# Second up projection as seven quarter products, with weight sums made by adding transfers

## The chip, the cores and the metric

One Trainium2 chip; the program runs on one of its cores. The metric is the device time of one execution in microseconds (us), less is better. Three runs of the kernel before gave a median of 1473.71 us (1473.31 to 1474.12).

The engines of the core are named as the profile names them: PE (TensorE, matmuls; PEld is its weight loads), DVE (VectorE), ACT (ScalarE), POOL (GpSimd) and SP (SyncE, which only issues transfers here). Each executes its own list of instructions in order and waits on semaphores for the others.

## What is computed

Two layers over 512 latent tokens and 256 context tokens of width 1024. Layer 0 mixes by a short gated convolution and a wide (31 taps) convolution module, layer 1 by windowed attention; each is followed by a ConvFFN. The change is in the ConvFFN of layer 1, which has latent tokens only. Cut to that:

```python
D_MODEL, SEQ, D_FF = 1024, 512, 2816

def conv_ffn(h, w_up, conv, w_down):
    u = dwconv(h @ w_up, conv)              # h: 512 x 1024, w_up: 1024 x 5632, conv: 3 taps per channel
    a, g = jnp.split(u, 2, axis=-1)
    return (jax.nn.silu(g) * a) @ w_down    # w_down: 2816 x 1024

x = x + g2 * conv_ffn(modulate(rmsnorm(x, norm_ffn[l]), sh2, sc2), w_up[l], w_conv_ffn[l], w_down[l])
```

All inputs are float32. In layer 0 the part that will matter is the wide convolution of the mixer: `u = v_b * sigmoid(gate_b)`, `dwconv(u, conv_b) + bias`, then a layer norm.

## The kernel before

**Layout.** Activations lie transposed: channels on the 128 partitions, tokens along the free dimension. A width of 1024 is eight k tiles. For accuracy every operand of a large matmul is split into a high and a low part (`split`, lines 157 to 160: ACT casts to the reduced type, DVE subtracts), and each product is three matmuls: low x high, high x low, high x high (`mm3`, lines 174 to 179). In the profile these are L177, L178 and L179.

**Weights.** `weights` (lines 162 to 168) has SP load a 128 x 1024 tile into one of three `wraw` buffers and splits it into `whi` and `wlo`. Loads run ahead as far as the three buffers let them.

**Second FFN** (`ffn` with l = 1). The inner width of 2816 is 22 pairs; pair f has an `a` tile and a `g` tile of the up projection. An up tile is 8 k tiles x 3 = 24 matmuls with 512 columns into one PSUM slot. There are eight slots (`turn` hands them out in turn). The first three pairs are computed half by half, while the tokens' halves are still being normalised (`side_by_side`, L208, L209 and L212). For each tile `conv3` applies the three taps (ACT L368, then DVE L370 twice), ACT takes silu of `g` (L704), DVE multiplies (L705) and `pair` splits the product into `gh` and `gl`. The pairs fall into five groups (`GROUPS`); after the first pair of the next group, `down` computes all eight tiles of the down projection for the group before, and `gate_in` (L360) adds each into `x`. The last group goes through `project`, which ends in the final norm. At the start of each FFN, `mod_rows` computes the modulation rows on DVE (`junk`, L254), from rows that SP loads.

**Layer 0.** `start` loads x and the modulation weights (`wmod`, line 222) and computes `h`. `glu` (lines 558 to 584) makes for each of four channel tiles j the padded input `ub`: POOL clears its three margins (line 568), DVE writes the body (line 570), ACT starts the convolution with tap 0 (`cacc`, line 575, which reads the margins), and 30 further taps follow on DVE (line 578). When tiles 0 and 1 are done POOL adds them into `cs` (line 584). `conv_norm` multiplies `cs` by a matrix of ones on PE (line 622) for the mean. `inverse` (lines 286 to 302) computes a reciprocal root, in most places on POOL (`ry`, L296).

**Order.** The program is written in source order; a scheduler then sets the order of each engine's list from the dependencies and from its own estimate of durations, so an instruction can be moved far from its place in the source. POOL issues no transfers in this kernel.

## Time and profile before

| what | value |
|---|---|
| median of three runs | 1473.71 us |
| profiled execution, its own time | 1473.53 us |
| its span (first to last instruction) | 1471.8 us |
| PE, busy share of the span | 98% |
| DVE, ACT, POOL | 70%, 41%, 3% |
| layer 0 up to its FFN | about 0 to 312 us |
| first FFN | about 312 to 836 us |
| attention | about 836 to 1072 us |
| second FFN, with the end of the attention's output | about 1072 to 1472 us |

An instruction's row has its start and duration; matmuls are pipelined, so the interval from one start to the next tells what one costs, not the duration of 0.28 or 0.39 us. In brackets stands the idle time of that engine before the instruction and what ended it. DMA share is the mean busy share of the core's 16 DMA engines. PEclk is the granted clock of PE, 1.00 being 2.4 GHz.

### The profile page before, as it was taken

How to read it: one execution, taken by the hardware profiler on the slowest of the kernel's cores; microseconds unless marked ns; L12 is line 12 of the kernel's file. 1: busy time of each engine (PE TensorE's matmuls, PEld its weight loads, DVE VectorE, ACT ScalarE, POOL GpSimd, SP SyncE). 2: the span in 40 equal slices, each digit the busy share in tenths (PEclk: the TensorE clock that was granted, in tenths of full speed). 3: DMA queues.
4: the chain of work that ended last, by engine and by line, in shares of the span. 5: the costliest groups of instructions: out<-in, count | busy, mean ns of one | idle time of the engine just before them, and what ended most of it. 6: DMA issues, size and time to landing. Idle time of an engine off the chain costs nothing.

```text
span 1471.8 us, 21937 instructions
## 1 busy us (share of the span) xinstructions
PE 1435.4 (98%) x8786; PEld 1228.8 (83%) x8786; DVE 1024.4 (70%) x1635; ACT 596.9 (41%) x983; POOL 47.8 (3%) x186
## 2 busy tenths in 40 slices
PE   5999999999999999999999999999999999999997
PEld 3888888888888888888888878768799888888887
DVE  6699998689977756456434689786676865655456
ACT  5421224463223223133123475786764442424245
POOL 0000001110000000000000110010001000000000
PEclk9999999999999999999999999999999999999999
DMA  9325433134544532333211324011155333233222
GB/s 374 111 70 173 158 115 130 31 113 146 168 132 127 186 106 81 120 125 91 81 47 43 106 91 125 14 40 58 42 174 163 90 112 98 84 114 97 94 80 74
DMA packets 52709, 161.25 MB, mean 110 GB/s; under 512 B 6400, under 2 KB 6528, under 8 KB 52480
## 3 DMA queue, kind: packets, MB, share of 16 engines
q1 hardware_dynamic: 52608, 159.87, 33.4%
q8 instruction: 68, 1.11, 0.3%
q14 instruction: 33, 0.27, 0.1%
HBM read 155.13 MB, written 2.10 MB: 107 GB/s over the span
## 4 chain that ended last, share of the span: by engine, by line
PE 91%; DVE 4%; ACT 2%; issue 1%; DMA 1%; POOL 1%; DVEq 0%; SPq 0%; ACTq 0%; POOLq 0%
PE slot L177 21%; PE slot L178 21%; PE slot L179 21%; PE av L178 3%; PE av L177 3%; PE av L179 3%; PE av L929 2%; PE pt L919 2%; PE s L900 2%; PE pt L179 2%; PE pt L178 2%; PE pt L177 2%; PE slot L226 1%; PE slot L212 1%; PE slot L208 1%
## 5 line engine op out<-in xcount | busy, mean ns | idle before, releaser
L177 PE MATMUL slot<-h,wlo 128*128 128x512 f32 (+1 forms) x1192 | 410.5, 346 | 2.2 <-DVE ub L570 1.2
L178 PE MATMUL slot<-h,whi 128*128 128x512 f32 (+1 forms) x1192 | 410.8, 345 | 0.2 <-DVE h L350 0.2
L179 PE MATMUL slot<-h,whi 128*128 128x512 f32 (+1 forms) x1192 | 410.8, 345 | 0.0
L159 ACT CAST whi<-wraw 128x1024 fp32r<-128x1024 f32 (+2 forms) x215 | 192.2, 902 | 208.5 <-PE slot L179 109.3
L177 PEld LDWEIGHTS slot<-h,wlo 128*128 128x128 f32 x1192 | 223.5, 188 | 34.3 <-issue 2.0
L178 PEld LDWEIGHTS slot<-h,whi 128*128 128x128 f32 x1192 | 224.1, 188 | 29.0 <-DVE h L350 0.5
L179 PEld LDWEIGHTS slot<-h,whi 128*128 128x128 f32 x1192 | 224.1, 188 | 27.6
L160 DVE TENSOR_TENSOR wlo<-wraw,whi 128x1024 fp32r<-128x1024 f32 (+2 forms) x215 | 222.2, 1040 | 25.1 <-ACT whi L159 24.6
L370 DVE SCALAR_TENSOR_TENSOR cf<-slot,par,cf 128x775 f32<-128x775 f32 (+1 forms) x132 | 122.7, 932 | 136.5 <-ACT cf L368 136.0
L177 PE MATMUL slot<-gh,wlo 128*128 128x512 f32 (+1 forms) x459 | 156.7, 342 | 0.7 <-DVE x L360 0.4
L178 PE MATMUL slot<-gl,whi 128*128 128x512 f32 (+1 forms) x459 | 155.5, 339 | 0.0
L179 PE MATMUL slot<-gh,whi 128*128 128x512 f32 (+1 forms) x459 | 155.1, 339 | 0.0
L368 ACT ACTIVATE cf<-slot,par 128x776 f32<-128x776 f32 (+1 forms) x66 | 55.3, 837 | 243.1 <-PE slot L179 230.7
L360 DVE SCALAR_TENSOR_TENSOR x<-slot,mod,x 128x256 f32<-128x256 f32 (+1 forms) x139 | 81.8, 618 | 73.6 <-PE slot L179 73.4
L578 DVE SCALAR_TENSOR_TENSOR cacc<-ub,par,cacc 128x783 f32<-128x783 f32 x120 | 118.6, 1040 | 0.2
L254 DVE CUSTOM_DVE_ANT_0 junk<-wmod,cb 128x1024 bf16<-128x1024 f32 x80 | 97.7, 1221 | 10.2 <-DMA wmod<-in_wmt 6.6
L177 PEld LDWEIGHTS slot<-gh,wlo 128*128 128x128 f32 x459 | 86.1, 188 | 12.0 <-DVE wlo L160 0.7
L178 PEld LDWEIGHTS slot<-gl,whi 128*128 128x128 f32 x459 | 86.4, 188 | 10.3 <-DVE mod L235 0.2
L179 PEld LDWEIGHTS slot<-gh,whi 128*128 128x128 f32 x459 | 86.4, 188 | 10.1
L907 DVE CUSTOM_DVE_ANT_0 sm<-s,mask,nsink 128x640 f32<-128x640 f32 (+1 forms) x58 | 46.8, 820 | 15.9 <-PE pt L919 12.4
L704 ACT ACTIVATE sgf<-cf 128x776 f32<-128x776 f32 (+1 forms) x44 | 32.7, 744 | 60.9 <-DVE cf L370 60.4
L910 ACT ACTIVATE sm<-sm,nm 128x513 f32<-128x513 f32 (+1 forms) x64 | 50.1, 786 | 10.6 <-DVE nm L907 5.6
(244 smaller groups left out, 2246.4 us busy)
## 6 DMA issues: line engine op xcount, KB each, us to landing
wraw<-in_w_up SPq DMA_DIRECT2D x88, 512.0 KB, 3.6
wmod<-in_wmt SPq DMA_DIRECT2D x56, 512.0 KB, 4.2
wmod<-in_wm SPq DMA_DIRECT2D x40, 512.0 KB, 5.3
wraw<-in_w_down SPq DMA_DIRECT2D x48, 256.0 KB, 2.6
wraw<-in_w_in SPq DMA_DIRECT2D x20, 512.0 KB, 4.0
wraw<-in_w_down SPq DMA_DIRECT2D x32, 320.0 KB, 2.9
wraw<-in_w_o SPq DMA_DIRECT2D x16, 512.0 KB, 3.4
wraw<-in_w_out SPq DMA_DIRECT2D x16, 256.0 KB, 3.4
```

What stands on the lines that cost most here:

```text
L159: self.act_mark = self.nc.scalar.copy(hi, src)
L160: self.mark = self.nc.vector.tensor_tensor(lo, src, hi.bitcast(F32), op=ALU.subtract)
L177: mm(out, lo, xh, start=first, stop=False)
L178: mm(out, hi, xl, start=False, stop=False)
L179: self.product = mm(out, hi, xh, start=False, stop=last)
L254: nc.vector.tensor_tensor_reduce(junk, w, self.cb[:, c, :], 1.0, 0.0, ALU.mult, ALU.add, col)
L360: self.nc.vector.scalar_tensor_tensor(self.x[k][:, lo:hi], acc, self.mod[:, l, chunk * 8 + k, c:c + 1], self.x[k][:, lo:hi], op0=ALU.mult, ...
L368: nc.scalar.activation(acc[:, :n], u[:, :n], AF.Copy, scale=w[:, 1:2])
L370: nc.vector.scalar_tensor_tensor(acc[:, o], u[:, i], w[:, j:j + 1], acc[:, o], op0=ALU.mult, op1=ALU.add)
L578: self.tapped = nc.vector.scalar_tensor_tensor(acc, ub[:, t:t + CB_N], w[:, t:t + 1], acc, op0=ALU.mult, op1=ALU.add)
L907: scored = nc.vector.tensor_tensor_reduce(sm[:, :n], s[:, SEQ - nl:SEQ + CTX], mk, -SCALE, nsink[:, hd:hd + 1], ALU.add, ALU.min, nm)
L910: self.scored = scored, nc.scalar.activation(sm[:, :n + 1], sm[:, :n + 1], AF.Exp, scale=-1.0, bias=nm, accum_out=z)
```

## The change

From pair 3 (`FEW`) on, the two up tiles of a pair (output halves `a` and `g`), the two halves of the k tiles (even and odd ones) and the two halves of the tokens are taken as a 2 x 2 block product. It is computed by seven products of quarters instead of eight (Strassen's scheme, in Winograd's form): each is 4 k tiles x 3 = 12 matmuls with 256 columns.

- **Sums of tokens.** `quarters` makes from the four quarters of `h` four sums (DVE L1112 to L1115) and splits them into `th` and `tl`. The unsplit `h` is kept for that (`raw`).
- **Sums of weights.** `weight_sums` makes for each of the 19 pairs four sums of weight quarters, `s1`, `s2`, `s4` and `s3`, in DRAM: a transfer from POOL copies one operand, a second one adds the other to it. That is 8 transfers of 128 x 512 floats a pair, 4 plain and 4 adding, 152 in all. In the source they stand in the first FFN, one step after each up tile (`next(sums, None)`).
- **Loads.** `load_seven` loads four `wraw` tiles per pair (seven quarters) instead of two; `next_seven` splits them.
- **Products.** `seven` accumulates the seven products in three PSUM slots, one of which is emptied four times, and assembles `ua` and `ug` in SBUF by copies on ACT and additions on DVE; `conv3` then reads these.
- **Down projection.** In layer 1 `down` is called one tile at a time; the table `DOWNS` spreads the 32 tiles over pairs 4 to 19, between the products.
- Eight instead of six pairs of `gh`, `gl` buffers; the weights of layer 1 are packed with even k tiles first.

```diff
+FEW = 3
+DOWNS = {
+    **{4 * grp + 4 + i: [(grp, 2 * i), (grp, 2 * i + 1)] for grp in range(3) for i in range(4)},
+    17: [(3, 0), (3, 1), (3, 2)], 18: [(3, 3), (3, 4), (3, 5)], 19: [(3, 6), (3, 7)],
+}
...
-                    self.ffn(1, HALVES, 6)
+                    self.ffn(1, HALVES, 8)
...
+    def weight_sums(self):
+        dma = self.nc.gpsimd.dma_start
+        w = self.a["w_up"][1]
+        add = dict(accum_op=ALU.add)
+        self.sums = {}
+        def pair(f):
+            a11, a21, a12, a22 = (w[f, i, :, j:j + 512] for i, j in ((0, 0), (0, 512), (1, 0), (1, 512)))
+            s1, s3 = (self.dram.tile([P, 512], F32, name=t, tag=f"{t}_{f}") for t in ("s1", "s3"))
+            s24 = self.dram.tile([P, 1024], F32, name="s24", tag=f"s24_{f}")
+            s2, s4 = s24[:, 0:512], s24[:, 512:1024]
+            self.sums[f] = s1, s24, s3
+            dma(s1, a21)
+            dma(s3, a11)
+            yield
+            dma(s1, a22, **add)
+            dma(s3, a21, **add)
+            yield
+            dma(s2, s1)
+            yield
+            dma(s2, a11, **add)
+            yield
+            dma(s4, s2)
+            yield
+            dma(s4, a12, **add)
+        under = []
+        todo = deque(range(FEW, NF))
+        while todo or under:
+            if todo:
+                under.append(pair(todo.popleft()))
+            under = [b for b in under if next(b, self) is None]
+            yield
+    def load_seven(self, f):
+        w = self.a["w_up"][1][f]
+        s1, s24, s3 = self.sums[f]
+        for parts in ((w[0][:, :512], s1), (s24,), (s3, w[1][:, :512]), (w[1][:, 512:],)):
+            raw, n = self.wts.tile([P, 1024], F32, name="wraw", tag="wraw", bufs=3), 0
+            for p in parts:
+                self.nc.sync.dma_start(raw[:, n:n + p.shape[1]], p)
+                n += p.shape[1]
+            yield raw[:, :n]
+    def next_seven(self, raws, out, first=False):
+        for i, raw in enumerate(raws):
+            if i == 0 and first:
+                for j in range(2):
+                    hi, lo = (self.ph.tile([P, SEQ], F32R, name=t, tag=f"{t}{4 + j}") for t in ("gh", "gl"))
+                    self.split(raw[:, 512 * j:512 * j + 512], hi, lo)
+                    out.append((hi, lo))
+            else:
+                if i == 3:
+                    hi, lo = (self.act.tile([P, DM], F32R, name=f"{t}2") for t in ("whi", "wlo"))
+                else:
+                    hi, lo = (self.wts.tile([P, 1024], F32R, name=t, tag=t, bufs=3) for t in ("whi", "wlo"))
+                n = raw.shape[1]
+                self.split(raw, hi[:, :n], lo[:, :n])
+                out.extend((hi[:, j:j + 512], lo[:, j:j + 512]) for j in range(0, n, 512))
+            yield
+    def seven(self, f, parts, h, then, early, late):
+        nc = self.nc
+        xa, va, ya = (self.slot()[:, :256] for _ in range(3))
+        ua, ug = (self.ph.tile([P, SEQ], F32, name=n, tag=f"{n}{f % 2}") for n in ("ua", "ug"))
+        q = lambda t, i: t[:, 256 * i:256 * i + 256]
+        b = {n: [(q(x[0], i), q(x[1], i)) for x in src] for n, src, i in (
+            ("11", h[0::2], 0), ("21", h[1::2], 0), ("22", h[1::2], 1),
+            *((n, list(zip(self.th, self.tl)), i) for i, n in enumerate(("n1", "t3", "n2", "t4"))))}
+        lo, hi = slice(0, 256), slice(256, 512)
+        def product(acc, w, n, start=False):
+            for k in range(4):
+                self.mm3(acc, w, k, *b[n][k], start and k == 0, k == 3, not start)
+        a11, s1, s2, s4, s3, a12, a22 = parts
+        product(xa, a11, "11", True)
+        nc.scalar.copy(ua[:, lo], xa)
+        product(va, s1, "n1", True)
+        nc.scalar.activation(ug[:, hi], va, AF.Copy, scale=-1.0)
+        then()
+        early()
+        product(xa, s2, "n2")
+        nc.scalar.copy(ua[:, hi], xa)
+        product(va, s4, "22")
+        nc.vector.tensor_tensor(ua[:, hi], ua[:, hi], va, op=ALU.add)
+        then()
+        product(ya, a12, "21", True)
+        nc.vector.tensor_tensor(ua[:, lo], ua[:, lo], ya, op=ALU.add)
+        product(xa, s3, "t3")
+        nc.vector.tensor_tensor(ug[:, hi], ug[:, hi], xa, op=ALU.subtract)
+        then()
+        late()
+        product(xa, a22, "t4")
+        nc.scalar.activation(ug[:, lo], xa, AF.Copy, scale=-1.0)
+        then()
+        return ua, ug
...
+        if l:
+            self.quarters()
 
         self.do(11 if l else 3)
         done = [self.slot() for _ in self.pre]
         self.side_by_side(done, h, segs)
         nf = len(done)
-        with self.tc.issue_after(self.marks[0].ins), self.tc.issue_after(self.marks[1].ins):
-            ahead = self.weights(a["w_up"][l, ups[nf][0], ups[nf][1]], into=self.spare(0))
+        if l == 0:
+            sums = self.weight_sums()
+            with self.tc.issue_after(self.marks[0].ins), self.tc.issue_after(self.marks[1].ins):
+                ahead = self.weights(a["w_up"][l, ups[nf][0], ups[nf][1]], into=self.spare(0))
+        else:
+            ahead = []
+            for _ in self.next_seven(self.load_seven(FEW), ahead, True):
+                pass
         g = []
 
         def up(f):
             nonlocal ahead
             acc = []
+            if l and f >= FEW:
+                now, ahead = ahead, []
+                then = self.next_seven(self.load_seven(f + 1), ahead) if f + 1 < NF else iter(())
+                head = deque(partial(down, *t) for t in DOWNS.get(f, ()))
+                fresh = any(f == grp[0] for grp in GROUPS)
+                early = lambda: [head.popleft()() for _ in range(0 if fresh else len(head) // 2)]
+                late = lambda: head and head.popleft()()
+                u = self.seven(f, now, h, lambda: next(then, None), early, late)
+                for t in head:
+                    t()
...
+                    next(sums, None)
...
-        def down(grp):
-            for m in range(KT):
-                w = self.weights(a["w_down"][l][grp][m], len(GROUPS[grp]) * P, self.spare(m % 3) if m % 3 < 2 else None)
-                s = self.slot()
-                self.wide_gemm(s, w, g[GROUPS[grp][0]:GROUPS[grp][-1] + 1], whole)
-                for lo, hi in whole:
-                    self.gate_in(m, s[:, lo:hi], l, 5, lo, hi)
-                if grp < 2:
-                    self.do(1)
+        def down(grp, m):
+            room = (self.spare(m % 3) if m % 3 < 2 else None) if l == 0 else self.late_room(m % 2)
+            w = self.weights(a["w_down"][l][grp][m], len(GROUPS[grp]) * P, room)
+            s = self.slot()
+            self.wide_gemm(s, w, [g[f] for f in GROUPS[grp]], whole)
+            for lo, hi in whole:
+                self.gate_in(m, s[:, lo:hi], l, 5, lo, hi)
+            if grp < 2:
+                self.do(1)
 
         for grp, fs in enumerate(GROUPS):
             for f in fs:
                 up(f)
 
-                if grp and f == fs[0]:
-                    down(grp - 1)
+                if l == 0 and grp and f == fs[0]:
+                    for m in range(KT):
+                        down(grp - 1, m)
...
+        self.raw = [self.shifted(self.act, "th", p, F32) for p in range(KT // 2)]
...
+    def quarters(self):
+        nc = self.nc
+        self.th, self.tl = [], []
+        for p, raw in enumerate(self.raw):
+            b = raw.rearrange("p (q n) -> p q n", q=4)
+            t, u = (self.tmp.tile([P, T], F32, name="qs", tag=g)[:, :SEQ] for g in ("tA", "tB"))
+            nc.vector.tensor_tensor(
+                t.rearrange("p (q n) -> p q n", q=2), b[:, 0:3:2, :], b[:, 1:2, :].broadcast_to([P, 2, 256]), op=ALU.subtract)
+            nc.vector.scalar_tensor_tensor(u[:, :256], t[:, :256], -1.0, b[:, 2, :], op0=ALU.mult, op1=ALU.subtract)
+            nc.vector.scalar_tensor_tensor(u[:, 256:], u[:, :256], -1.0, b[:, 3, :], op0=ALU.mult, op1=ALU.subtract)
+            hi, lo = self.quarter_room(p)
+            for i, src in enumerate((t, u)):
+                self.split(src, hi[:, 512 * i:512 * i + 512], lo[:, 512 * i:512 * i + 512])
+            self.th.append(hi)
+            self.tl.append(lo)
...
+    even_odd = d["w_up"][1, FEW:].reshape(NF - FEW, 2, P, KT // 2, 2, P).transpose(0, 4, 2, 1, 3, 5)
+    d["w_up"][1, FEW:] = even_odd.reshape(NF - FEW, 2, P, DM)
```

What the scheduler makes of it differs from the source at the following places.

POOL, from its start. Before, the clearing of the margins of `ub` and the sum `cs` are its first work after constants:

```order
L1057 UNCONDITIONAL_BRANCH [waits barrier_Pool_Activation_PE_DVE_SP_gather]
L568 MEMSET ub_594 128x15 [waits DMAHW3_49,DMAHW2_49,PE_49]
L568 MEMSET ub_594 128x15 x2
L568 MEMSET ub_673 128x15 [waits DMAHW2_49,DMAHW1_49]
L568 MEMSET ub_673 128x15 x2
L568 MEMSET ub_810 128x15 [waits DMAHW7_49,DMAHW6_49]
L568 MEMSET ub_810 128x15 x2
L568 MEMSET ub_948 128x15 [waits DMAHW5_49]
L568 MEMSET ub_948 128x15 x2
L584 ISA
L584 TENSOR_TENSOR cs_681<-cacc_600,cacc_679 128x783 [waits DMAHW0_49,DVE_49]
```

After, POOL's list begins with the transfers of the weight sums (L680, L681, L686 and L690 copy, L683, L684, L688 and L692 add). DMASW0 to DMASW7 are the eight semaphores of POOL's transfers; each row that waits for one waits for the transfer eight places earlier. These are the last four of the 72 that stand before the clearing, and the first after it:

```order
L684 DMA s3_4447<-in_w_up 128x512 [waits DMASW4_49]
L683 DMA s1_4521<-in_w_up 128x512 [waits DMASW5_49]
L686 DMA s24_3365<-s1_3363 128x512 [waits DMASW6_49]
L684 DMA s3_4522<-in_w_up 128x512 [waits DMASW7_49]
L576 MEMSET ub_596 128x15 [waits DMAHW3_49,DMAHW2_49,PE_49]
L576 MEMSET ub_596 128x15 x2
L576 MEMSET ub_675 128x15 [waits DMAHW2_49,DMAHW1_49]
L576 MEMSET ub_675 128x15 x2
L576 MEMSET ub_812 128x15 [waits DMAHW7_49,DMAHW6_49]
L576 MEMSET ub_812 128x15 x2
L576 MEMSET ub_950 128x15 [waits DMAHW5_49]
L576 MEMSET ub_950 128x15 x2
```

80 more follow, and behind the last of them stands `cs`:

```order
L692 DMA s24_4960<-in_w_up 128x512 [waits DMASW5_49]
L692 DMA s24_5040<-in_w_up 128x512 [waits DMASW6_49]
L692 DMA s24_5113<-in_w_up 128x512 [waits DMASW7_49]
L592 ISA
L592 TENSOR_TENSOR cs_683<-cacc_602,cacc_681 128x783 [waits DMAHW0_49,DVE_49]
L304 TENSOR_SCALAR ry_2120<-rv_2119 128x4 [waits Activation_49]
```

All 152 transfers have moved from the first FFN to ahead of the layer 0 work on POOL.

DVE, at the start of the second FFN. Before, the splits of the second half of `h` are followed at once by the modulation rows (`junk`):

```order
L336 TENSOR_TENSOR xr_10319<-x7_72,r_10253 128x256
L160 TENSOR_TENSOR h_9908<-ht_10309,h_9907 128x256
L160 TENSOR_TENSOR h_9910<-ht_10315,h_9909 128x256
L160 TENSOR_TENSOR h_9912<-ht_10321,h_9911 128x256
L254 ISA junk_10334,mod_90<-wmod_10332,cb_10329 128x1024
```

After, the quarters' sums and splits (20 instructions, the last six here) stand between, and the split of the weight sums `s2`, `s4` (`wlo_10911`) comes after two of the modulation rows:

```order
L1114 SCALAR_TENSOR_TENSOR qs_10564<-qs_10563,th_10079 128x256
L1115 SCALAR_TENSOR_TENSOR qs_10564<-qs_10564,th_10079 128x256
L167 TENSOR_TENSOR tl_10558<-qs_10552,th_10557 128x512
L167 TENSOR_TENSOR tl_10558<-qs_10553,th_10557 128x512
L167 TENSOR_TENSOR tl_10569<-qs_10563,th_10568 128x512
L167 TENSOR_TENSOR tl_10569<-qs_10564,th_10568 128x512
L262 ISA junk_10577,mod_92<-wmod_10575,cb_10528 128x1024
L262 ISA mod_92 128x1
L262 ISA junk_10581,mod_92<-wmod_10579,cb_10528 128x1024
L262 ISA mod_92 128x1
L167 TENSOR_TENSOR wlo_10911<-wraw_10908,whi_10910 128x1024
```

The splits of `h` themselves stand between the first of these sums; what follows them on DVE has moved back by the quarters.

## Rows read from the trace of the kernel before

**Rows 1.** The page: engine totals, then slices (PEclk, DMA share, GB/s).

```profile
PE 1435.4 (98%) x8786; PEld 1228.8 (83%) x8786; DVE 1024.4 (70%) x1635; ACT 596.9 (41%) x983; POOL 47.8 (3%) x186
...
PEclk9999999999999999999999999999999999999999
DMA  9325433134544532333211324011155333233222
```

**Rows 2.** Windows, layer 0: PE, PEld, DVE, ACT, POOL busy; PEclk, DMA share, GB/s.

```profile
0.00:57.00 57.00, 39.01 (x412) 31.10 (x413) 32.39 (x62) 32.08 (x48) 0.76 (x16) 1.00 0.77 293
10.00:37.00 27.00, 19.01 (x247) 14.13 (x248) 20.09 (x39) 15.17 (x25) 0.00 (x0) 1.00 1.03 409
57.00:218.00 161.00, 159.85 (x1230) 137.66 (x1229) 154.13 (x168) 40.11 (x54) 1.89 (x1) 1.00 0.36 124
70.00:190.00 120.00, 120.00 (x923) 103.41 (x922) 116.67 (x128) 27.75 (x36) 0.00 (x0) 1.00 0.38 131
```

**Rows 3.** Tile `ub`: durations min/median/max in ns, first and last start.

```profile
L578 DVE SCALAR_TENSOR_TENSOR cacc<-ub,par,cacc x120: 1022/1030/2006, 61.7 to 222.1; 128x783 f32<-128x783 f32 x120
...
L575 ACT ACTIVATE cacc<-ub,par x4: 1040/1045/1047, 60.3 to 104.4; 128x783 f32<-128x783 f32 x4
```

**Rows 4.** Timelines of SP's queue and POOL: start, duration, instruction, idle before and releaser.

```profile
0.74 3.32 SPq L121 DMA_DIRECT2D x<-in_x  x7
...
42.76 0.56 POOL L568 MEMSET ub<- 128x15 f32 x12 [42.32 <-PE slot L226]
191.01 1.89 POOL L584 TENSOR_TENSOR cs<-cacc 128x783 f32<-128x783 f32 x1 [147.69 <-DVE cacc L578]
237.03 0.20 POOL L296 TENSOR_SCALAR ry<-rv 128x4 int32<-128x4 int32 x1 [44.14 <-ACT rv L294]
```

**Rows 5.** Tile `cs`: its reader on PE.

```profile
L622 PE MATMUL slot<-cs,ones x4: 380/538/592, 218.4 to 250.7; 128*128 128x512 f32 x2, 128*128 128x256 f32 x2
```

**Rows 6.** Timeline of PE, second FFN: an up tile of 512 columns.

```profile
1307.53 0.39 PE L179 MATMUL slot<-gh,whi 128*128 128x512 f32 x1
...
1309.57 0.39 PE L179 MATMUL av<-h,whi 128*128 128x512 f32 x1
```

**Rows 7.** Timeline of PE: 256 columns, first FFN, then end of the second.

```profile
601.31 0.28 PE L177 MATMUL slot<-gh,wlo 128*128 128x256 f32 x1
...
602.01 0.28 PE L177 MATMUL slot<-gh,wlo 128*128 128x256 f32 x1
...
1431.07 0.28 PE L179 MATMUL pt<-gh,whi 128*128 128x256 f32 x1
...
1433.47 0.28 PE L178 MATMUL pt<-gl,whi 128*128 128x256 f32 x1
```

**Rows 8.** Lines by form, second FFN: count, busy us, mean ns, idle before.

```profile
L160 DVE TENSOR_TENSOR wlo<-wraw,whi 128x1024 fp32r<-128x1024 f32 x50 | 60.8, 1221 | 10.3 <-ACT whi L159 10.2
L160 DVE TENSOR_TENSOR gl<-sgf,gh 128x512 fp32r<-128x512 f32 x22 | 15.2, 692 | 9.0 <-ACT gh L159 9.0
L254 DVE CUSTOM_DVE_ANT_0 junk<-wmod,cb 128x1024 bf16<-128x1024 f32 x8 | 9.8, 1225 | 6.8 <-DMA wmod<-in_wmt 4.8 <-ACT cb L666 1.9
L336 DVE TENSOR_TENSOR xr<-x,r 128x256 f32<-128x256 f32 x16 | 6.6, 423 | 2.3 <-ACT r L528 1.7 <-ACT ht L348 0.5
...
L159 ACT CAST whi<-wraw 128x1024 fp32r<-128x1024 f32 x33 | 34.5, 1045 | 22.1 <-DMA wraw<-in_w_up 19.3 <-PE slot L179 2.7
```

**Rows 9.** Windows, second FFN, with the columns of rows 2.

```profile
1110.00:1160.00 50.00, 49.49 (x294) 43.31 (x293) 40.15 (x70) 26.88 (x44) 0.00 (x0) 1.00 0.38 116
1160.00:1440.00 280.00, 280.00 (x1273) 233.36 (x1272) 158.99 (x207) 98.54 (x138) 0.00 (x0) 1.00 0.31 97
```

**Rows 10.** Timelines of DVE and ACT, start of the second FFN.

```profile
1119.35 0.42 DVE L160 TENSOR_TENSOR h<-ht,h 128x256 fp32r<-128x256 f32 x1 [0.78 <-ACT h L159]
...
1129.95 0.69 ACT L368 ACTIVATE cf<-slot,par 128x512 f32<-128x512 f32 x1 [8.26 <-PE slot L212]
```

More of the change, by code (lines that the diff above doesn't have):

```diff
@@ L604, in pair @@
     def pair(self, j, src, n, width):
+        if j > 5 and width == SEQ:
+            t = self.ph.tile([P, 2, SEQ], F32R, name="gp", tag=("cb", "wmod")[j - 6])
+            self.split(src[:, :n], t[:, 0, :], t[:, 1, :])
+            return t[:, 0, :], t[:, 1, :]
         gh = self.ph.tile([P, -(-width // P) * P], F32R, name="gh", tag=f"gh{j}")
@@ L692, in up @@
                     s = done[i]
+                elif l:
+                    s = u[part]
                 else:
```

40 lines of the change are left out of this document (28 added, 12 removed).

## The prediction

> **What bounds the kernel now.** I read the head of the page first: TensorE (PE) is busy for 98% of the span and runs at full granted clock in nearly every slice, so time leaves this kernel only by giving PE less to do, and any wait put on it is paid in full [rows 1]. The second reading is the DMA line of the same page: the sixteen DMA engines are near idle for most of the span, but full in the first slice [rows 1]. The windows of layer 0 show that in detail: from 10 to 37 us their share is 1.03 at 409 GB/s, which is all that they give; from 57 to 218 us it is 0.36 [rows 2]. In the same view VectorE (DVE) is busy for 116.67 of the 120 us between 70 and 190, so in that stretch it sets the pace beside PE; this is the 120 tap instructions of the wide convolution, first at 61.7 us, last at 222.1 us [rows 2, 3]. Third, GpSimd (POOL): it does almost nothing (3% [rows 1]), but what it does is needed: the margins of `ub` are cleared at 42.76 us, `cs` is summed at 191.01 us, and the reciprocal root starts at 237.03 us [rows 4]. The ScalarE instruction that opens each convolution reads the cleared tile, at 60.3 us for the first [rows 3]; the tap on DVE follows it. `cs` is read by PE at 218.4 us [rows 5].
>
> **The products.** Before, a pair of up-projection tiles is 2 x 8 x 3 = 48 matmuls of 512 columns. In the steady part of the second FFN one starts every 0.2267 us (from 1307.53 to 1309.57 us there are nine) [rows 6]. After, a pair is 7 x 4 x 3 = 84 matmuls of 256 columns. These start 0.1167 us apart in layer 0 (601.31 to 602.01, six) and 0.1200 apart at the end of the second FFN (1431.07 to 1433.47, twenty) [rows 7]. For 19 pairs: before 19 x 48 x 0.2267 = 206.8 us, after 19 x 84 x 0.1167 = 186.3 or x 0.1200 = 191.5. The gain is 20.5 or 15.3 us; I take 18. It is less than the eighth that the count of columns promises, because half the columns cost more than half the time.
>
> **What feeds the products.** Per pair DVE splits 3.5 instead of 2 full weight tiles (1.5 x 1.22 us) and adds three half-width results (3 x 0.42): 3.1 us more [rows 8]. From 1160 to 1440 us it is busy for 159 of 280 us [rows 9]; with 17 pairs there 53 us more, 212 of some 265: that hides. ScalarE gets 1.5 x 1.05 us of casts and four short copies more per pair, and is at 98.5 of 280 [rows 8, 9]: hidden too. The four uses of one PSUM slot per pair put PE behind the copy that empties it, but the order has another product or a down tile between. I allow 0.2 us a pair, 4 us, between 0 and 1 us a pair (19); no row shows that wait.
>
> The quarters cost DVE at a bad place. Per pair of k tiles: one 512-wide difference (0.69), two 256-wide (0.42 each), two 512-wide splits (0.69 each), 2.9 us; four of these, 11.6 us [rows 8]. Before, the last split of `h` starts at 1119.35 us, and the first up tile is complete and read from PSUM at 1129.95 [rows 10]; PE is covered until then. After, DVE ends the quarters near 1119.8 + 11.6 = 1131.4, then has two `junk` reductions (1.23 each [rows 8]) queued ahead of the weight split that the second product waits for, so PE waits some 5 us, and the stretch from 1110 to 1160, where DVE is busy for 40.15 of 50 us [rows 9], overflows by a few more. I take 8 us, between 3 and 14. The second FFN thus gives -18 + 8 + 4 = **-6 us**, between -17 (20.5 less 3) and +18 (14 and 19 less 15.3). Spreading the down tiles leaves their count and shape as they are: nothing on the sum; it is what fills the gaps between products.
>
> **The weight sums, and where they land.** Written in the first FFN, the 152 adding and copying transfers depend on inputs alone, and the order shows that on POOL they stand first of all: 72 of them ahead of the clearing of `ub`, all 152 ahead of `cs`. From the ninth on each waits for the one eight places earlier, and POOL executes in order; so the clearing waits until nearly all of the 72 have landed. Behind the clearing on POOL are 80 transfers, then `cs` and every reciprocal root. Behind it on ScalarE stand the weight casts that follow the first convolution, on DVE the taps; and PE runs out of split weights two or three tiles later.
>
> What does one transfer cost? It writes 128 x 512 x 4 = 262 KB of DRAM; no row shows a DRAM to DRAM transfer. From below: it takes the engines as long as a load of its size at the saturated rate, 0.262 MB at 409 GB/s = 0.64 us [rows 2]. From above: the engines pay for each stream apart, so a copy (one read, one write) is 1.28 us and an add (two reads, one write) 1.92. I take 1.28 for both: a copy has to read and write on the DRAM side, an add to read twice. The other loads go on: up to 57 us they moved 57 x 293 GB/s = 16.7 MB, 40.7 us of the engines at 409 GB/s [rows 2]. The first loads are issued from 0.74 us on, 0.47 us apart (3.32/7) [rows 4]; I take 1.6 us for the first bytes. The 72 transfers (42 copies, 30 adds) are 92 us, so the clearing comes at 1.6 + 40.7 + 92 = 134.5 us, and the instruction at 60.3 us moves by **+74 us**. With 0.64 it comes at 88.4 (+28), with 1.28 and 1.92 at 153.7 (+93). The slower opening loads lie inside that wait, since all of them share the same engines. DVE has no slack afterwards, so the taps, and all that follows, move by as much.
>
> What is late next is `cs`. The other 80 transfers take 102 us, and the loads from 57 to 218 us (161 x 124 GB/s = 20.0 MB) 49 us [rows 2]: POOL is free at 134.5 + 102 + 49 = 286 us. `cs` must start 1.9 us before 218.4, that is 216.5 + 74 = 290.5 us: just in time. At the dear prices (34 copies, 46 adds, 132 us) POOL is free at 153.7 + 132 + 49 = 334 us where 309.5 is due: 25 us more, +118 in all. By the time of the first FFN all sums are done, so nothing collides there.
>
> The Trainium skill, "DMA: Bandwidth & Descriptors", section "Latency and other measured facts", gives some 207 to 214 GB/s per direction for copies between HBM tensors. By that an estimate of one transfer is 1.25 us and the clearing comes at 132 us; no run here shows it yet. The same page, section "Issuing engines are not separate DMA queues", says that transfers started by GpSimd run on the same 16 engines as SyncE's and interleave; if they did not, the cheap rival below would hold.
>
> **The sum.** The profiled execution took 1473.53 us (span 1471.8), beside a median of 1473.71. 1473.5 + 74 - 6 = **1542 us**.
>
> **Rivals.** (1) Cheap transfers: 0.64 us each, the clearing at 88 us, 1473.5 + 28 - 6 = 1496 us. For it: reads and writes of an engine may overlap, as they do in a load. Against: an add reads twice. (2) Dear adds and a second wait, PE held once for `ub` and once for `cs`: 1473.5 + 118 - 6 = 1586 us. (3) POOL is slowed in writing the transfers' descriptors while DVE works: DVE is busy for 32 us before 57 us [rows 2]; if POOL did nothing in those, the clearing comes 32 us later, 1574 us. The Trainium skill, "SBUF — State Buffer", section on who interferes with whom, has such a lock for some DVE modes; I give it little, since while `ub` is awaited DVE stands still. (4) The other side, faster: the transfers are gone before `ub` is due. The 72 would have to land by some 66 us (60.3 and the 6 us gained); while the opening loads need 40.7 us of the engines, that leaves 0.33 us for each, half of the cheap price. Then only the second FFN's gain is left: 1473.5 - 6 = 1467 us. It decides wherever a DRAM to DRAM transfer does not take the time of the engines that the profile counts. (5) A second FFN held up on DVE for all 22 pairs, +18 instead of -6: 24 us on any of these.
>
> **How the numbers follow.** The forecast with one wait of 50 to 100 us (1517 to 1567): 0.50. Cheap (1): 0.16. Second wait (2): 0.18. Descriptors (3): 0.05. Faster (4): 0.08. A cheap transfer that meets a bad second FFN or so, near 1473: 0.03, of which 0.02 within 0.2% (3 us, about what a measurement of this kernel tells from no change) and 0.01 above. Ends of the sum: 1473.5 + 28 - 17 = 1485 and 1473.5 + 118 + 18 = 1610. Without the corners, and leaving out (4): 1488 to 1600. Slower 0.90, same 0.02, faster 0.08.
>
> **What would show it.** POOL's timeline: the clearing of `ub` near 135 us instead of 42.76, with DMA waits ahead of it, and `cs` near 290. ScalarE waits for POOL at the first `cacc`; PE stands idle for some 70 us between 60 and 140, and its granted clock falls there. DMA share near 1 until about 285 us. The first FFN as before in length. In the second, products 0.117 to 0.120 us apart, a gap of some 5 us near its start, and DVE near 80%. The forecast is wrong if the clearing stays before 66 us (cheap or separate transfers), or if the wait for `cs` is the longer one.

## The result, and the profile after

The changed kernel takes 1546.36 us (median of four runs, 1545.41 to 1553.06) against 1473.51 us (four runs, 1472.25 to 1474.12): 1.0505 times as long, 95% interval 1.0475 to 1.0536, a loss of 73 us. The forecast was 1542. The loss is in layer 0, as forecast, and the transfers cause it. Two sizes in the working were wrong and cancelled: the delay at the first convolution was smaller than forecast, and a delay behind it, forecast as nothing, was there.

The page of the changed kernel: engine totals, the granted clock and the DMA share in 40 slices of 38.6 us, and the row of POOL's transfers (packets, MB, share of the 16 engines' span).

```profile
PE 1441.8 (93%) x9470; PEld 1260.1 (82%) x9470; DVE 1085.2 (70%) x1751; ACT 652.4 (42%) x1106; POOL 149.1 (10%) x338
...
PEclk9788998999999999999999999999999999999999
DMA  9999998422345353334321132310215555454442
...
q0 software_dynamic: 17024, 39.86, 11.4%
```

Beside [rows 1], PE has fallen from 98% to 93%, and where one slice of the DMA line was full, six are now and a seventh nearly. The 152 transfers cost 11.4% of 1544.1 us, 176 us of the engines, **1.16 us each** (the forecast took 1.28).

The timeline of POOL, columns as in [rows 4], around the clearing of `ub` and around `cs`:

```profile
116.39 0.81 POOL L684 DMA_DIRECT2D s<-in_w_up  x1 [0.75 <-issue]
116.92 0.89 POOL L576 MEMSET ub<- 128x15 f32 x12
118.48 0.56 POOL L686 DMA_DIRECT2D s<-s  x1 [0.67 <-issue]
...
257.36 0.81 POOL L692 DMA_DIRECT2D s<-in_w_up  x1 [3.79 <-issue]
257.99 2.13 POOL L592 TENSOR_TENSOR cs<-cacc 128x783 f32<-128x783 f32 x1
```

The clearing stands right behind the 72 transfers, as the order said, at 116.92 us instead of 42.76, and `cs` behind the last of the 152. What reads them (tile `ub`, columns as in [rows 3]; tile `cs`; then the first matmul of the first FFN):

```profile
L586 DVE SCALAR_TENSOR_TENSOR cacc<-ub,par,cacc x120: 1025/1050/1070, 118.5 to 273.3; 128x783 f32<-128x783 f32 x120
...
L583 ACT ACTIVATE cacc<-ub,par x4: 1038/1042/1045, 117.4 to 160.6; 128x783 f32<-128x783 f32 x4
...
L635 PE MATMUL slot<-cs,ones x4: 377/486/593, 294.5 to 321.3; 128*128 128x512 f32 x2, 128*128 128x256 f32 x2
...
L216 PE MATMUL slot<-h,wlo x112: 277/283/680, 368.3 to 1205.1; 128*128 128x256 f32 x72, 128*128 128x512 f32 x40
```

The first convolution has moved from 60.3 to 117.4 us (+57), the last tap from 222.1 to 273.3 (+51), PE's reading of `cs` from 218.4 to 294.5 (+76), the start of the first FFN from 294.6 to 368.3 (+74). So the delay shrinks during the taps and grows again behind them, although `cs` has been ready since 260.1 us. PE's waits (total, times, longest), first up to 370 us, then those from 190 to 260 us alone:

```profile
PE slot L234 <- DMA wmod<-in_wm: 22.5, 11, 6.3
PE slot L299 <- DVE ss L292: 20.1, 1, 20.1
PE slot L185 <- DVE ub L578: 19.1, 2, 17.9
PE slot L185 <- DVE wlo L167: 6.0, 3, 3.6
...
PE slot L234 <- DMA wmod<-in_wm: 6.3, 3, 2.9
PE slot L185 <- DVE wlo L167: 3.6, 1, 3.6
PE slot L185 <- DVE ya L609: 2.0, 1, 2.0
```

No wait is for `cs`. The longest sum is for the modulation weights `wmod`, which SP loads; but 16.2 of its 22.5 us lie before 110 us, ahead of the first convolution. Behind the clearing, from 190 to 260 us, `wmod` accounts for 6.3 us and DVE, which is then still in its taps, for 5.6. The first wait, for `ss`, is 20.1 instead of 14.5 us long, because `x` is loaded later. The windows of layer 0 (columns as in [rows 2]):

```profile
0.00:57.00 57.00, 22.12 (x182) 14.27 (x182) 21.07 (x44) 16.81 (x23) 22.77 (x42) 0.88 1.01 359
57.00:110.00 53.00, 44.98 (x336) 36.89 (x334) 14.78 (x22) 18.22 (x28) 21.04 (x29) 0.94 1.02 271
110.00:130.00 20.00, 4.17 (x10) 3.31 (x11) 11.33 (x13) 3.72 (x4) 9.89 (x24) 0.50 0.94 163
130.00:190.00 60.00, 57.21 (x378) 49.58 (x377) 60.00 (x66) 14.22 (x17) 24.29 (x36) 0.99 0.99 249
190.00:260.00 70.00, 56.62 (x453) 45.86 (x452) 67.32 (x73) 12.32 (x18) 28.35 (x38) 0.93 1.03 266
260.00:294.00 34.00, 34.00 (x287) 28.26 (x287) 16.86 (x21) 7.48 (x13) 0.12 (x1) 0.94 0.48 156
```

In the first 57 us PE is busy for 22.12 us where it was 39.01 [rows 2]: 17 us are lost before the clearing is due at all. From 110 to 130 us it stands still for the clearing; the clock there is 0.50, the lower level of 1.2 GHz. From 190 to 260 us, with the clearing long done, it is again idle for 13 of 70 us beside a DMA share of 1.03, and from 260 to 294 us it has no gap: it comes late to `cs` because it still has other work ahead of it.

The whole of layer 0 up to the first FFN, before and after:

```profile
0.00:294.60 294.60, 272.76 (x2049) 230.54 (x2049) 244.23 (x333) 104.39 (x164) 13.47 (x56) 1.00 0.41 145
```

```profile
0.00:368.30 368.30, 291.86 (x2048) 240.09 (x2048) 244.90 (x333) 105.91 (x164) 116.97 (x208) 0.93 0.80 224
```

PE is idle for 76.4 instead of 21.8 us, and the same matmuls are recorded as busy for 19.1 us longer, at a mean clock of 0.93 instead of 1.00. So of the 74 us some 55 are waits. How much of the other 19 is the lower clock is not separated.

After layer 0 the two kernels run alike. In 524 us of the first FFN, before (from 312 us) and after (from 386 us), PE is busy for the same time:

```profile
312.00:836.00 524.00, 523.58 (x3040) 462.25 (x3039) 335.51 (x457) 153.12 (x193) 0.00 (x0) 1.00 0.35 110
```

```profile
386.00:910.00 524.00, 523.58 (x3042) 462.42 (x3040) 335.50 (x457) 152.48 (x192) 0.00 (x0) 1.00 0.35 110
```

The last matmul of the columns computed half by half into a slot starts at 1206.5 instead of 1129.7 us (+77), the span ends at 1544.1 instead of 1471.8 (+72): the second FFN itself gains 4 to 5 us, and 3 us are lost between the start of the first FFN and that point. In its first part PE waits four times (0.51, 1.00, 2.23 and 3.34 us) while DVE has no gap:

```profile
1206.50:1240.00 33.50, 26.43 (x191) 25.62 (x190) 33.47 (x54) 19.84 (x33) 0.00 (x0) 0.90 0.64 213
1240.00:1510.00 270.00, 268.99 (x1890) 252.10 (x1890) 207.13 (x299) 145.46 (x243) 0.00 (x0) 1.00 0.49 152
```

The third of these waits, the matmuls at the lower clock that follow it, and the fourth wait:

```profile
1218.59 0.39 PE L185 MATMUL slot<-h,wlo 128*128 128x256 f32 x1 [2.23 <-DVE wlo L167]
...
1219.56 0.42 PE L186 MATMUL slot<-h,whi 128*128 128x256 f32 x1
...
1222.55 0.42 PE L185 MATMUL av<-th,wlo 128*128 128x256 f32 x1
...
1236.58 0.58 PE L185 MATMUL slot<-th,wlo 128*128 128x256 f32 x1 [3.34 <-DVE ug L763]
```

### The profile page after: what moved, and what is told of

It reads as the page before. It is cut to its first block, busy times and chain, and to the rows that moved or that the text cites. A ratio compares the mean times of both kernels' runs of the same rounds, so it can differ in the third digit from the quotient of the medians.

```text
span 1544.1 us, 23964 instructions
## 1 busy us (share of the span) xinstructions
PE 1441.8 (93%) x9470; PEld 1260.1 (82%) x9470; DVE 1085.2 (70%) x1751; ACT 652.4 (42%) x1106; POOL 149.1 (10%) x338
## 3 DMA queue, kind: packets, MB, share of 16 engines
q0 software_dynamic: 17024, 39.86, 11.4%
## 4 chain that ended last, share of the span: by engine, by line
PE 73%; DVE 11%; issue 7%; POOL 4%; DMA 3%; ACT 2%; SPq 0%; DVEq 0%; ACTq 0%; POOLq 0%
PE slot L185 17%; PE slot L186 17%; PE slot L187 17%; DVE cacc L586 5%; PE av L1083 2%; PE pt L1073 2%; DVE wlo L167 2%; PE s L1054 2%; PE av L185 2%; PE av L186 2%; PE av L187 2%; PE pt L185 1%; PE pt L187 1%; PE pt L186 1%; DMA wraw<-in_w_down 1%
## 5 line engine op out<-in xcount | busy, mean ns | idle before, releaser
L185 PE MATMUL slot<-h,wlo 128*128 128x256 f32 (+1 forms) x1152 | 388.2, 339 | 35.2 <-DVE ub L578 19.1
L186 PE MATMUL slot<-h,whi 128*128 128x256 f32 (+1 forms) x1152 | 388.9, 338 | 0.1
L187 PE MATMUL slot<-h,whi 128*128 128x256 f32 (+1 forms) x1152 | 387.8, 337 | 0.0
L166 ACT CAST whi<-wraw 128x1024 fp32r<-128x1024 f32 (+2 forms) x249 | 220.0, 892 | 238.3 <-PE slot L187 94.0
L167 DVE TENSOR_TENSOR wlo<-wraw,whi 128x1024 fp32r<-128x1024 f32 (+2 forms) x249 | 255.6, 1031 | 79.7 <-ACT whi L166 78.9
L378 DVE SCALAR_TENSOR_TENSOR cf<-slot,par,cf 128x775 f32<-128x775 f32 (+1 forms) x92 | 92.8, 1012 | 109.8 <-ACT cf L376 109.7
L185 PE MATMUL slot<-gh,wlo 128*128 128x512 f32 (+1 forms) x419 | 142.2, 342 | 2.3 <-DVE wlo L167 1.0
L186 PE MATMUL slot<-gl,whi 128*128 128x512 f32 (+1 forms) x419 | 141.7, 339 | 0.0
L187 PE MATMUL slot<-gh,whi 128*128 128x512 f32 (+1 forms) x419 | 141.4, 338 | 0.0
L376 ACT ACTIVATE cf<-slot,par 128x776 f32<-128x776 f32 (+1 forms) x46 | 41.4, 901 | 200.5 <-PE slot L187 196.4
L185 PEld LDWEIGHTS slot<-gh,wlo 128*128 128x128 f32 x419 | 78.4, 188 | 11.9 <-DVE wlo L167 1.2
```

Of the source, the lines that this page charges most:

```text
L166: self.act_mark = self.nc.scalar.copy(hi, src)
L167: self.mark = self.nc.vector.tensor_tensor(lo, src, hi.bitcast(F32), op=ALU.subtract)
L185: mm(out, lo, xh, start=first, stop=False)
L186: mm(out, hi, xl, start=False, stop=False)
L187: self.product = mm(out, hi, xh, start=False, stop=last)
L376: nc.scalar.activation(acc[:, :n], u[:, :n], AF.Copy, scale=w[:, 1:2])
```

## The experiments

The theory at the start: the transfers cost 74 us in layer 0 because they stand there on POOL and fill the DMA engines, the second FFN gains little. Its rivals: the transfers cost as much anywhere; or the second FFN or the moved instructions are to blame.

**Transfers behind layer 0.** They are tied behind the last reciprocal root of layer 0 on POOL.

```diff
-            eng.tensor_tensor(y, t, y, op=ALU.mult)
+            root = eng.tensor_tensor(y, t, y, op=ALU.mult)
+        if eng is nc.gpsimd:
+            self.root = root
...
-                    next(sums, None)
+                    with self.tc.issue_after(self.root.ins):
+                        next(sums, None)
```

> The change whole, but the 152 transfers stand on POOL behind the last reciprocal root of layer 0 instead of at the head of its list. Theory (layer 0 pays for the place of the transfers on POOL and for the share of the DMA engines that they take there; the second FFN gains little): clearing of ub at about 43 us, first FFN starts at about 294.5 us as before, and with the -1.4 us that the traces give for all after that, 1472 us (1469 to 1478); the transfers, 1.16 us of the engines each by the page of the changed kernel, take 176 us of engine time and fit beside the first FFN's loads, which use a share of 0.35. Rival A (the transfers cost as much wherever they stand, because loads of weights come late beside them): 1490 to 1520, with PE waiting for DMA or for split weights in the first FFN. Rival B (layer 0 is not slowed by them): about 1545 as with the whole change.

Measured: 1470.26 us (9 runs), ratio 0.9978 (0.9968 to 0.9989). The windows of layer 0's end and of the first FFN:

```profile
294.00:312.00 18.00, 17.35 (x77) 14.00 (x78) 15.31 (x31) 13.09 (x23) 9.55 (x22) 1.00 0.56 178
312.00:400.00 88.00, 88.00 (x534) 78.65 (x533) 76.34 (x113) 34.02 (x47) 35.10 (x52) 1.00 1.04 293
400.00:500.00 100.00, 100.00 (x581) 88.26 (x580) 74.04 (x104) 27.12 (x34) 38.88 (x56) 1.00 1.03 272
500.00:600.00 100.00, 100.00 (x581) 88.27 (x580) 65.02 (x91) 26.08 (x33) 24.64 (x35) 1.00 0.85 247
```

The DMA engines are as full here, share 1.04, as they were in layer 0, and PE does not lose a microsecond. So a full DMA share alone is not the loss. The rows suggest what makes the difference: in the kernel before, the loads of the first FFN come at 110 GB/s, a tile of 512 KB in some 4.8 us, while a `wmod` tile of the same size keeps PE busy for 0.62 us (16 matmuls). A load that takes longer is felt where PE uses a tile up quickly; no run isolates this. The first convolution is back at 60.3 us, the first FFN starts at 294.3. All that the change does outside layer 0 is worth 3.2 us (1.6 to 4.7), by the ratio.

**Clearing on DVE**, and nothing else. `nc.gpsimd.memset` of the margins becomes `nc.vector.memset`.

> The change whole, but DVE clears the margins of ub, so that the first convolution does not wait for POOL; cs and the reciprocal roots still stand behind all 152 transfers. Theory: the 57 us at the first convolution go; taps end near 225 to 235 us, but cs cannot be summed before POOL is free at about 258 us, so PE waits there until about 260 instead of reading cs at 218: 1473.5 + 42 - 1.4 = 1514 us (1500 to 1530). Rival (full DMA engines are the whole cost, POOL's order is none): 1540 to 1550. Rival (the clearing is the whole cost): 1475 to 1495.

Measured: 1520.96 us (one run), inside the range of the theory, but not by its course. The first convolution starts at 88.7 us, still 28 us late, and the last tap at 245.8. PE does wait for `cs`, but for 1.01 us only, at 272.15 us, where some 42 us were expected:

```profile
272.15 1.12 PE L635 MATMUL slot<-cs,ones 128*128 128x512 f32 x2 [1.01 <-POOL cs L592]
```

**POOL with transfers alone.** Clearing, `cs` and reciprocal roots of layer 0 all on DVE.

```diff
-        y = self.inverse(ss, chunks, ones2, o[:, segs[0][0] - off:segs[0][0] - off + 2 * n], eng or nc.gpsimd)
+        y = self.inverse(ss, chunks, ones2, o[:, segs[0][0] - off:segs[0][0] - off + 2 * n], eng or (nc.gpsimd if hasattr(self, "sums") else nc.vector))
...
-            nc.gpsimd.memset(ub[:, lo:lo + n], 0.0)
+            nc.vector.memset(ub[:, lo:lo + n], 0.0)
...
-            self.taps[1].append(lambda: nc.gpsimd.tensor_tensor(self.cs, self.cacc[0], acc, op=ALU.add))
+            self.taps[1].append(lambda: nc.vector.tensor_tensor(self.cs, self.cacc[0], acc, op=ALU.add))
```

> The change whole, but the clearing, cs and the reciprocal roots of layer 0 all run on DVE, so POOL has nothing but transfers there. Theory: only the late loads are left (wmod and w_in beside full DMA engines until about 260 us), which the trace of the changed kernel puts at about 17 us after the first convolution and some 20 before it that had been hidden in the wait for the clearing: 1473.5 + 17 to 37 - 1.4 = 1489 to 1509 us, I take 1500. Rival (POOL's order alone): 1472 to 1478.

Measured: 1522.77 us (one run), above the range and no better than with `cs` left on POOL. Its tile `ub`, the start of its first FFN and PE's waits up to 350 us:

```profile
L583 ACT ACTIVATE cacc<-ub,par x4: 1045/1045/1045, 88.0 to 133.4; 128x783 f32<-128x783 f32 x4
...
L216 PE MATMUL slot<-h,wlo x112: 277/283/632, 345.8 to 1181.8; 128*128 128x256 f32 x72, 128*128 128x512 f32 x40
...
PE slot L234 <- DMA wmod<-in_wm: 22.5, 13, 6.0
PE slot L299 <- DVE ss L292: 20.2, 1, 20.2
```

With nothing waiting for POOL, the first convolution is still 28 us late and the first FFN 51 us. The theory in its first form falls: POOL's order costs only what is left of the 74 us, some 22; late loads cost the larger part.

**Transfers alone.** The kernel before with `weight_sums` added and its generator advanced in the first FFN; nothing reads the sums.

> The kernel before with the 152 transfers alone; nothing reads the sums, and the second FFN is the old one. Theory: layer 0 pays the whole 74 us by itself, 1473.5 + 74 = 1547 us (1540 to 1553), first FFN from about 368 us. Rival (part of the loss comes from the second FFN or from the moves of other instructions that the new code brings): under 1535.

Measured: 1554.34 us (one run), 1 us above the range, clearing at 116.6 us, first FFN at 373.1. Layer 0 pays all of it without any of the new second FFN; the 8 us above the changed kernel are 5 us of a later first FFN in this one execution, and the gain that the old second FFN lacks.

**Adds as copies.** `add = dict(accum_op=ALU.add)` becomes `add = dict()`, so the second operand overwrites the first.

> The change with the 76 adding transfers as plain copies, so the weights that the products use are not the sums: it prices an add against a copy. The page of the changed kernel gives 11.4% of 16 engines for 152 transfers, 1.16 us each. Theory (an add costs what a copy costs, as the forecast took it): the share of the transfers' queue stays near 11.4%, the clearing of ub stays near 117 us, the time near 1546. Rival (an add is 1.5 times a copy): copies 0.93 us each, the share falls to about 9.2%, the clearing of ub comes some 12 to 14 us earlier (103 to 105 us), the time is 1520 to 1537.

Measured: 1514.27 us (one run). The queue of the transfers, and the clearing and first convolution:

```profile
q0 software_dynamic: 12160, 39.86, 7.5%
...
L576 POOL MEMSET ub<- x12: 129/130/132, 90.0 to 90.5; 128x15 f32 x12
...
L583 ACT ACTIVATE cacc<-ub,par x4: 1035/1042/1045, 91.4 to 136.8; 128x783 f32<-128x783 f32 x4
```

7.5% of 1512.5 us over 152 is **0.75 us a copy**; the 76 adds are then (176.0 - 76 x 0.746) / 76 = **1.57 us each**, 2.1 times a copy, more than the rival's 1.5. The packets agree in kind: 80 for a copy (12160 / 152), 144 for an add ((17024 - 76 x 80) / 76). By these prices the 72 transfers are 42 x 0.746 + 30 x 1.57 = 78 us, and 1.6 + 40.7 + 78 = 121 us is near the measured 116.92. At 91.4 us the first convolution is 3 us later than with POOL free of all but (adding) transfers: with copies the order seems to cost little, a comparison of two kernels and not a run of its own, and yet 41 us are lost.

**A sixteenth of the bytes.** The transfers keep number and place but carry 32 columns; the second FFN reads plain quarters.

```diff
-        dma = self.nc.gpsimd.dma_start
+        dma = lambda out, src, **kw: self.nc.gpsimd.dma_start(out[:, :32], src[:, :32], **kw)
...
-        s1, s24, s3 = self.sums[f]
+        s1, s24, s3 = w[0][:, 512:], w[1], w[0][:, 512:]
```

> The change with 152 transfers in the same places on POOL, but of 32 columns instead of 512, a sixteenth of the bytes; the second FFN reads plain quarters of the weights in place of the sums. Theory after the runs so far (the bytes on the DMA engines are the cost, and POOL's order costs only because the bytes take long): POOL issues a transfer in 0.52 to 0.85 us, so the clearing of ub comes at 42 to 65 us, the first convolution at 60 to 66, cs long before 216, the first FFN starts at 294 to 300, 1470 us (1467 to 1478). Rival (the number of transfers and the waits for the transfer eight places earlier are the cost): clearing at 75 to 110 us, 1485 to 1520 us.

Measured: 1475.32 us (one run; 1471.97 for the kernel before on that chip).

```profile
L576 POOL MEMSET ub<- x12: 313/1040/1042, 70.2 to 71.5; 128x15 f32 x12
...
L583 ACT ACTIVATE cacc<-ub,par x4: 1027/1044/1047, 71.4 to 105.8; 128x783 f32<-128x783 f32 x4
...
L216 PE MATMUL slot<-h,wlo x112: 277/283/795, 298.6 to 1135.5; 128*128 128x256 f32 x72, 128*128 128x512 f32 x40
```

With the same number of transfers in the same places, nearly all of the loss is gone: what costs is the time that the bytes take on the DMA engines (the transfers' queue now has 2.1% of 1473.5 us, 31 us instead of 176). The clearing came between the two theories, later than the first and earlier than the rival: issuing takes POOL 0.5 to 0.85 us a transfer, and some 27 of the 70 us are gaps between them. But a first convolution 11 us late made the first FFN only 4 us late. A delay there does **not** pass one to one.

**Transfers behind the clearing.** POOL clears first and issues the transfers from 43 us on; `cs` and roots on DVE as above.

```diff
-            nc.gpsimd.memset(ub[:, lo:lo + n], 0.0)
+            self.cleared = nc.gpsimd.memset(ub[:, lo:lo + n], 0.0)
...
-                    next(sums, None)
+                    with self.tc.issue_after(self.cleared.ins):
+                        next(sums, None)
```

> The change whole, but POOL clears the margins of ub first and issues all 152 transfers behind that (from about 43 us on), and cs and the reciprocal roots of layer 0 run on DVE. So the opening loads are undisturbed, and the DMA engines are full from about 43 to some 280 us. Theory (loads that come late cost at two places: 28 us before the first convolution, 23 us between it and the first FFN, by the kernel with POOL free): first convolution at 60.3 as before, first FFN at 294.5 + 23 = 318, 1470 + 23 = 1493 us (1485 to 1502). Rival 1 (only the opening loads cost): 1470 to 1475. Rival 2 (the same engine time is paid for wherever it falls in layer 0): 1515 to 1525.

Measured: 1499.05 us (one run). First convolution at 60.3 us, first FFN at 321.6 (+27). Its windows:

```profile
57.00:110.00 53.00, 51.85 (x322) 45.59 (x324) 50.77 (x56) 16.00 (x18) 23.32 (x35) 1.00 0.96 228
110.00:190.00 80.00, 77.94 (x607) 65.03 (x599) 76.52 (x83) 16.74 (x23) 30.40 (x46) 1.00 1.00 286
190.00:300.00 110.00, 93.26 (x591) 74.22 (x590) 74.21 (x132) 30.16 (x54) 42.86 (x59) 0.94 1.02 255
```

Both rivals fall. In the kernel before, PE is busy for 51.85, 80.00 and 106.99 us in these three stretches. So beside a full DMA share nothing is lost from 57 to 110 us, 2 us up to 190, and 14 us from 190 to 300, where PE waits for `wmod` (7.2 us), for the sums over `cacc` (3.9) and for the norm's `rd` (3.5), and the clock is 0.94.

These three kernels take the parts of the loss away one after the other. By the start of the first FFN: whole change 368.3; POOL's order out, 345.8; late opening loads out too, 321.6; all transfers out of layer 0, 294.3. So order is **22 us**, opening loads **24**, later loads **27**. In another sequence the shares may differ, and the two in the middle are kernels that were run once.

**A late clearing without transfers.** The kernel before, with 92 additions of a scratch tile on POOL ahead of the clearing.

> The kernel before, with POOL kept busy by 92 additions of a scratch tile ahead of the clearing of ub, and no transfers: the cost of a late clearing by itself. It should be cleared at about 115 us (92 x about 1.24, scaled from 1.89 for 783 columns). Theory of the forecast (DVE has no slack after the first convolution, so the delay passes one to one): the first convolution moves from 60.3 to about 116, the first FFN from 294.5 to 350, 1473.5 + 56 = 1529 us. Rival (the layer has slack, since a late clearing costs only 22 us beyond what late loads cost, by the kernel with POOL free of all else): the first FFN at 315 to 335, 1495 to 1513 us.

Measured: 1549.79 us (one run), and of no use for the question. The clearing came at 127.67 us, but ACT started all four convolutions together at 151.86: the scheduler had put them behind other work, presumably because it counts POOL's additions as long. All taps then ran in one stretch, and PE waited for `cs`:

```profile
151.86 1.97 ACT L583 ACTIVATE cacc<-ub,par 128x783 f32<-128x783 f32 x2
...
296.97 2.08 PE L630 MATMUL slot<-cs,ones 128*128 128x512 f32 x2 [40.88 <-POOL cs L592]
```

What a late clearing costs by itself is known only from the 11 us of the small transfers.

**No transfers at all.** The changed kernel without them; its products read plain quarters.

> The change without the 152 transfers: the products read plain quarters of the weights in place of the sums. Everything else, the loads of the second FFN included, is as in the change. Theory (beside the first FFN the transfers cost nothing): the same as with the late transfers, 1470 us (1467 to 1473); the difference from 1473.4 is the whole gain of the products less what the second FFN loses at its start. Rival (the late transfers cost a few us in the first FFN or leave the sums late): 1462 to 1466.

Measured: 1468.08 us (5 runs), ratio 0.9967 (0.9954 to 0.9980); the interval overlaps that of the late transfers. The medians are 2 us apart, and by the two intervals the 152 transfers beside the first FFN could cost up to some 4. The traces put it lower: the profiled executions have the same span, 1469.8 us, and in both the last half-by-half columns come 836 to 837 us behind the start of the first FFN.

**Modulation rows in the first FFN.** The late transfers, and the rows of the second FFN's gate (`junk`) reduced at the end of the first.

```diff
-            self.mod_rows(1, 16, 24, 1)
+            self.mod_rows(1, 16, 32, 1)
...
-        self.do(11 if l else 3)
+        self.do(0 if l else 3)
```

(With it, `cb`, its silu and the two `mod_rows` calls ahead are made for l = 0 only.)

> The late transfers, and the eight modulation rows that DVE reduces at the start of the second FFN (junk) moved to the end of the first FFN. Theory (the second FFN loses 7 us of waits and 3 us of clock at its start because DVE has more than it can do between 1206 and 1240 us of the changed kernel, and 8 x 1.3 us of that are these rows): the waits at its start fall to some 1 to 3 us, 1462 us (1459 to 1466). Rival (PE waits there for weight loads or for PSUM slots, not for DVE's list): 1468 to 1472. The rows cost nothing in the first FFN, where DVE is busy for 335 us of 524.

Measured: 1464.61 us (4 runs), ratio **0.9940** (0.9924 to 0.9957), below both the kernel before and the changed one. The 35 us after the last half-by-half columns, with late transfers, and with the rows moved too:

```profile
1131.50:1166.50 35.00, 29.61 (x214) 27.42 (x213) 34.65 (x54) 20.70 (x34) 0.00 (x0) 0.95 0.66 216
```

```profile
1131.00:1166.00 35.00, 30.42 (x232) 28.51 (x231) 33.59 (x49) 26.21 (x44) 0.00 (x0) 1.00 0.51 159
```

In the same 35 us PE gets through 232 instead of 214 matmuls; its longest wait is 1.3 instead of 2.2 us, and the clock stays at 1.00. The step on DVE's list is right in kind. It is not the whole: waits of 0.8 to 1.3 us for ACT's copies `ua` and for casts took part of its place, so 5.7 us were gained, not 8.

## Why the prediction was right, and where it was not

**Place and sign.** The order was read rightly: 72 transfers ahead of the clearing, 152 ahead of `cs`, and the loss is layer 0's. The kernel with late transfers shows it from the other side.

**The price of a transfer** was 1.28 us for both kinds; it is 0.75 for a copy and 1.57 for an add, 1.16 in the mean. A copy is near the lower price, 0.64, at which reads and writes overlap; an add is between the forecast's 1.28 and the dear 1.92. The estimate of 1.25 us for one transfer does not hold for copies: 262 KB in 0.746 us is 351 GB/s. It was worked out from the rate that the Trainium skill gives in "DMA: Bandwidth & Descriptors", section "Latency and other measured facts", 207 to 214 GB/s for rows of 16 KiB at large pitches. The rows here are of 2 KB, a layout that the section has no rate for; the measurement decides. The clearing came at 117 us instead of 134.5, and POOL was free at 258 instead of 286.

**"The slower opening loads lie inside that wait"** holds for the sum, since the clearing comes last in the changed kernel: the first convolution follows it within 0.5 us. But it hides that these loads are a cause of their own. With POOL out of the way the first convolution is still 28 us late, so undoing POOL's order alone saves some 22 of the 74 us.

**"DVE has no slack afterwards, so the taps, and all that follows, move by as much"** is the first step that failed. DVE's 97% between 70 and 190 us [rows 2] left room: 57 us at the first convolution were 51 at the last tap, and 11 us were 4 at the first FFN. A stretch that is almost full for one engine is not full for the path.

**"What is late next is `cs`"** is the second. `cs` was ready at 260 us, 34 us before PE came to it. PE itself was late: from 190 to 260 us it waited for `wmod` and for DVE, and then it had no gap until it came to `cs`. In the kernel whose transfers stand behind the clearing, 27 us were lost behind the first convolution while the engines were full. The working had asked when POOL is free, not when SP's loads land beside POOL's transfers; the DMA share of 0.36 between 57 and 218 us [rows 2] was counted as room for the transfers, and never as loads with a deadline. Forecast were 74 us at the first convolution and none behind it, measured 57 and 17, and the sum came out right: that it did so within 5 us is luck.

The sign that PE would stand idle for some 70 us between 60 and 140 us did not come either. From 57 to 130 us it was idle for 24 (by the windows above); the rest of its waits were spread over the opening loads and the time behind 190 us.

**The products.** The timeline of PE after gives 24 matmuls of 256 columns from 1223.06 to 1225.86 us, 0.117 each, as forecast; the median of the stage is 0.120. From 1130 us on PE's busy time is 333.88 us before (29.49 + 280.00 + 24.39 in windows to 1160, 1440 and 1472), 322.49 with late transfers (29.61 + 266.49 + 26.39, to 1165, 1435 and 1470) and 317.68 with the rows moved too (30.42 + 268.26 + 19.00, to 1165, 1435 and 1463): 11 to 16 us less. Busy time also holds matmuls at the lower clock. By the starts alone, the mean of 1100 intervals behind a matmul of 256 columns from 1240 to 1440 us is 0.1185 us; 19 x 84 of them are 189.1 us against 206.8, a gain of 17.7 where 18 was taken. So the products were sized rightly. **What feeds them** was put at 8 + 4 us; the waits from 1206 to 1240 us are 7.1 us, of which 4.3 are for copies and additions that empty a PSUM slot (1.00 for ACT's `ug`, 3.34 for DVE's), and the lower clock costs some 3 more. So the second FFN's -6 was measured as -3.2 (-1.6 to -4.7), inside its range.

**The rivals.** The forecast's own interval of 1517 to 1567 us holds the time. The dear second wait for `cs` did not come. That DVE would hold up the writing of descriptors is not seen: in the first FFN POOL issues at a DMA share of 1.04 while DVE is busy for 76.34 of 88 us.

## What to carry to other kernels

Work that depends on inputs alone has no place of its own: a scheduler may put it at the very front, where the opening loads are, so tie it to the stage in which the DMA engines have room and PE does not wait for fresh loads. The same 176 us of transfers cost 73 us beside layer 0, whose PE used some loads up quickly, and nothing that the trace shows beside the first FFN (2 us by the medians). When pricing a shared resource, list first the loads with a deadline in that stretch, then the queue in which the new work stands.

## What the runs showed of the hardware

- A DRAM to DRAM transfer of 262 KB takes the 16 engines 0.75 us when it copies (the kernel with adds as copies) and 1.57 us when it adds (worked out with the changed kernel's share), with 80 and 144 packets. In the changed kernel POOL's instruction that issues one takes 0.52 to 0.56 us in the median for a copy and 0.82 to 0.83 for an add.
- Beside its own transfers POOL's other work is slower: a clearing of 15 columns took 112 ns before, 387 ns in the changed kernel and 1040 ns among the small transfers (medians). With copies in place of the adds it took 130 ns.
- In the kernel with a busy POOL, DVE's additions of two SBUF operands were slower while POOL added: 1618 instead of 967 ns for 776 columns. The Trainium skill, "SBUF — State Buffer", section "Who interferes with whom", says that a DVE instruction with two SBUF inputs contends with a GpSimd instruction that reads SBUF; this agrees.
- In the changed kernel, after waits of 1.00 and 2.23 us, PE fell to its lower clock of 1.2 GHz from 1219.56 to about 1222.8 us (256 columns in 0.21 instead of 0.12 us), which cost some 1.5 us on top of the waits; after the wait of 3.34 us the same came from 1236.6 to 1239.9 us.
